# S5 scan with a rotation table of three planes, 512-column operations and states copied by ScalarE

## The chip, the cores and the metric

One core of a Trainium2 chip runs the whole program in one launch. The time is the device time of one execution in microseconds; for the kernel before, the median of three executions. A few per cent of a stretch's instructions may be missing in a trace, and starts and durations are those of one profiled execution.

## The reference

One inference step of a decoder trunk with four layers. The token mixers are S5 (layers 0 and 3), stick-breaking attention (layer 1) and a chunked gMLP (layer 2); behind each comes a SwiGLU FFN, and every sub-layer stands between two RMSNorms. A prompt of 512 positions and 8 sample tokens share all weights; the model has 1024 channels, and all values are fp32. The change concerns the S5 mixer alone:

```python
def s5_mixer(xn, w_in, lam_re, lam_im, log_dt, b_re, b_im, c_re, c_im, d_skip, w_glu, h0_re, h0_im):
    u = xn @ w_in                                  # 64 groups of 16 channels, 64 complex states each
    dt = exp(log_dt)
    ar, ai = exp(lam_re * dt) * cos(lam_im * dt), exp(lam_re * dt) * sin(lam_im * dt)
    br, bi = ...                                   # discretised b applied to u
    hr, hi = associative_scan(h[t] = a * h[t - 1] + b[t])          # complex, over the positions
    y = hr @ c_re - hi @ c_im + d_skip * u
    val, gate = split(gelu(y) @ w_glu)
    return val * sigmoid(gate), hr[-1], hi[-1]
```

## The kernel before

The class `Trunk` holds activations as 8 tiles of 128 channels x 520 columns (512 prompt positions, 8 sample tokens). A matmul with weights is made of three products in a reduced fp32 format (lines L235, L236, L238): the weights are loaded from DRAM (`raw`), ScalarE rounds them to `wh` (L206) and VectorE or GpSimd makes the rest `wl` (L208). These matmuls are most of the program. The instructions of every engine stand in a fixed order, which a scheduler writes with a timeline model of its own; in the source, tasks such as the S5 pipeline are generators that yield a number of microseconds of TensorE work (`S5Y`, `PREPY`, `STASH`) or a condition, and so are woven into the weight matmuls.

**S5.** `s5` (L994) projects the input; `u_evict` brings each tile of u out of PSUM (L1008, L1011) and copies its 8 sample columns to the end (L1012). `s5_pipe` (L786) then takes the 8 channel tiles through a pipeline. The 512 positions are cut into 64 chunks of 8. Stages of one tile:

- `powers_b` on GpSimd (L809 to L811; the first tile on VectorE), `powers_c` half on VectorE and half on GpSimd (L835 to L837): products of b and c with the powers of a inside a chunk (`ba`, `ca`). `kernels` (L839) makes the in-chunk kernel, writes it to one of two padded buffers `kpad`, stores it as `dk` (L854) and loads it back in shifted form as `wn` (L858).
- `inputs`: loads the tile's rotation table `rot` from DRAM (L862), spreads rho (L864), and makes the chunk weights `wi` from `ba` (matmuls L879, ScalarE L882).
- `chunks`: stores u (`du`, L887) and loads it in chunk form (`uq`, L890).
- `scan` (L894): 32 matmuls (L901) give the real and imaginary input of the 64 chunks for 4 blocks of 128 states in PSUM. VectorE multiplies them by the cosine (L909) and by the sine with real and imaginary part exchanged (L910), 512 columns each; combines them per part (L913, 256 columns each); runs a scan with real decay per part (L915); rotates back per part (L919, L920); and writes the states to `hm`, in four operations of 64 partitions x 256 columns (L925), while ScalarE copies the initial states there (L924). GpSimd takes the last states out (L926).
- `outputs` (L933, L934, ScalarE `ys` L938) and `finish` (L946, GELU into `zt` L950, then `xh` L393 and `xl` L394 for the GLU matmul).

In layer 0 all of this runs in the pipeline. For layer 3 (`kept`) `s5_stash` (L714) makes `wi`, `ca` and `wn` ahead, inside layer 2's FFN, and keeps them in DRAM; its pipeline loads them (L866 to L870). The `rot` tile in SBUF has one buffer in layer 0 and two in layer 3.

**Tables.** `s5_prep` (L603) makes the rotation table in 8 blocks of 4 state blocks, 64 columns each: an angle (VectorE L704 to L707), then ScalarE Abs (L708) and two Sin (L709, L710) for sine and cosine, in a tile `ro` with three buffers; each block is stored to DRAM (`rotd`, L711). Layer 0's tables are made at the start of the program, layer 3's inside the gMLP.

## Time and profile before

| | us |
|---|---|
| three executions | 2747.35, 2749.26, 2748.29 |
| median | 2748.29 |
| profiled execution | 2746.49 |
| its span, first to last instruction | 2744.8 |
| TensorE busy | 2576.6 (94%) |
| VectorE busy | 1545.9 (56%) |
| ScalarE busy | 1012.0 (37%) |
| GpSimd busy | 459.1 (17%) |
| mean granted TensorE clock | 0.968 of full speed |

The profiled execution is a single one, and its span is 1.7 us shorter than its own time. Busy shares are means over stages with different limits: what an engine's work is worth is read from the stretch in which it lies. The page cuts the span in 40 slices of 68.6 us (tenths of busy time, 9 is 90% or more); the first S5 layer's pipeline lies in the second and third slice, the second's in the 32nd and 33rd.

```profile
PE   7769999999998899999999989999999889999998
DVE  8883553434647854734345778565646755634344
ACT  5443333222344454432223564433324333432222
POOL 5661210000128820300000203000001111200000
```

PE is TensorE, DVE VectorE, ACT ScalarE and POOL GpSimd. SP in the orders below is SyncE, which issues the DMAs.

### The profile page before, as it was taken

Reading aid. Unit: us, or ns where it says so; the run is one execution under the profiler, and the core shown is the slowest. Engines: PE = TensorE matmul, PEld = TensorE weight load, DVE = VectorE, ACT = ScalarE, POOL = GpSimd, SP = SyncE. Lnnn points to the kernel's source line nnn. Section 1 sums busy time; section 2 is a strip of 40 time slices with the busy share of each in tenths; the row PEclk is TensorE's granted clock in tenths of the full one; section 3 lists DMA queues with packets and bytes.
Section 4 is the critical chain, followed back from the end, with each engine's and each line's share of the span. In section 5 each row is a group of like instructions: output and inputs, shape, how many; then the busy total and the mean of one; then the engine's idle time right before and its main releaser. Section 6 shows DMA issues by size and latency. Waiting matters only on the chain.

```text
span 2744.8 us, 49994 instructions
## 1 busy us (share of the span) xinstructions
PE 2576.6 (94%) x20922; PEld 2457.4 (90%) x20922; DVE 1545.9 (56%) x2703; ACT 1012.0 (37%) x1713; POOL 459.1 (17%) x487
## 2 busy tenths in 40 slices
PE   7769999999998899999999989999999889999998
PEld 6659999999986667999999889999999779999998
DVE  8883553434647854734345778565646755634344
ACT  5443333222344454432223564433324333432222
POOL 5661210000128820300000203000001111200000
PEclk8879999999999999999999999999999999999999
DMA  4533223333147643233333333344333544233331
GB/s 118 146 87 90 80 80 106 93 93 91 41 134 243 222 147 93 66 103 94 93 92 63 90 101 90 114 135 141 116 110 123 167 129 124 66 104 92 90 90 46
DMA packets 483073, 295.48 MB, mean 108 GB/s; under 512 B 52296, under 2 KB 458080, under 8 KB 482848
## 3 DMA queue, kind: packets, MB, share of 16 engines
q1 hardware_dynamic: 473632, 258.73, 33.1%
q0 software_dynamic: 9216, 33.56, 3.5%
q8 instruction: 165, 2.70, 0.4%
q14 instruction: 60, 0.49, 0.1%
HBM read 262.51 MB, written 29.72 MB: 106 GB/s over the span
## 4 chain that ended last, share of the span: by engine, by line
PE 73%; DVE 11%; DMA 5%; ACT 4%; POOL 3%; issue 2%; SPq 0%; ACTq 0%; DVEq 0%; POOLq 0%
PE pp L235 22%; PE pp L236 22%; PE pp L238 22%; POOL kp L1190 1%; DVE wl L208 1%; DMA raw<-in_w_ffn_in_dram 1%; DVE pn L423 1%; DVE x L425 1%; ACT wh L206 1%; PE pp L1338 1%; PE pp L1334 1%; DVE hm L925 1%; POOL x L425 1%; DMA rot<-rotd 1%; DMA wn<-wnd 1%
## 5 line engine op out<-in xcount | busy, mean ns | idle before, releaser
L235 PE MATMUL pp<-xh,wh 128*128 128x264 f32 (+1 forms) x4480 | 1209.0, 288 | 26.5 <-DVE u L1008 6.0
L236 PE MATMUL pp<-xl,wh 128*128 128x264 f32 (+1 forms) x4480 | 1210.6, 286 | 6.6 <-DVE xl L408 6.4
L238 PE MATMUL pp<-xh,wl 128*128 128x264 f32 (+1 forms) x4480 | 992.7, 286 | 6.2 <-POOL wl L208 5.6
L235 PEld LDWEIGHTS pp<-xh,wh 128*128 128x128 f32 x4480 | 853.5, 191 | 40.9 <-issue 14.1
L236 PEld LDWEIGHTS pp<-xl,wh 128*128 128x128 f32 x4480 | 854.5, 191 | 11.9 <-DVE xl L408 9.7
L206 ACT ACTIVATE wh<-raw 128x1024 fp32r<-128x1024 f32 (+2 forms) x384 | 391.3, 1023 | 1080.4 <-PE pp L236 724.7
L238 PEld LDWEIGHTS pp<-xh,wl 128*128 128x128 f32 x4480 | 738.7, 191 | 9.7 <-POOL wl L208 5.8
L208 DVE TENSOR_TENSOR wl<-raw,wh 128x1024 fp32r<-128x1024 f32 (+2 forms) x364 | 442.6, 1218 | 292.8 <-ACT wh L206 290.2
L236 PE MATMUL pp<-hl,wh 128*128 128x256 f32 (+1 forms) x1408 | 377.2, 283 | 0.0
L235 PE MATMUL pp<-hh,wh 128*128 128x256 f32 (+1 forms) x1408 | 376.7, 284 | 0.0
L238 PE MATMUL pp<-hh,wl 128*128 128x256 f32 (+1 forms) x1408 | 312.9, 283 | 0.0
L235 PEld LDWEIGHTS pp<-hh,wh 128*128 128x128 f32 x1408 | 265.1, 188 | 1.2 <-issue 1.2
L236 PEld LDWEIGHTS pp<-hl,wh 128*128 128x128 f32 x1408 | 265.3, 188 | 0.0
L238 PEld LDWEIGHTS pp<-hh,wl 128*128 128x128 f32 x1408 | 230.7, 188 | 0.0
L1622 DVE TENSOR_TENSOR tg<-pp,rs 128x520 f32<-128x520 f32 (+2 forms) x100 | 62.5, 632 | 215.4 <-PE pp L238 215.3
L1633 DVE TENSOR_TENSOR tg<-pp,tg 128x520 f32<-128x520 f32 (+2 forms) x96 | 62.4, 652 | 209.2 <-PE pp L238 208.6
L1645 DVE TENSOR_TENSOR op<-pp,op 128x520 f32<-128x520 f32 (+2 forms) x96 | 54.0, 563 | 168.1 <-PE pp L238 167.9
L340 POOL TENSOR_TENSOR acc<-acc,s 128x256 f32<-128x256 f32 (+1 forms) x96 | 83.7, 872 | 99.2 <-ACT s L336 95.3
L208 POOL TENSOR_TENSOR wl<-raw,wh 128x1024 fp32r<-128x1024 f32 x20 | 48.2, 2414 | 303.6 <-ACT wh L206 274.4
L407 ACT ACTIVATE xh<-x,gt 128x264 fp32r<-128x264 f32 (+1 forms) x128 | 63.0, 505 | 60.8 <-DVE x L425 42.5
L408 DVE SCALAR_TENSOR_TENSOR xl<-x,gt,xh 128x264 fp32r<-128x264 f32 (+1 forms) x128 | 76.7, 615 | 1.4 <-ACT xh L407 1.2
L336 ACT ACTIVATE sq<-op 128x256 f32<-128x256 f32 (+2 forms) x72 | 32.6, 453 | 101.4 <-DVE op L1645 68.4
...
## 6 DMA issues: line engine op xcount, KB each, us to landing
...
```

Source lines behind the costliest of these rows:

```text
L206: nc.scalar.activation(wh[:, :nk], raw[:, :nk], AF.Copy)
L208: on.tensor_tensor(wl[:, :nk], raw[:, :nk], wh[:, :nk], op=ALU.subtract)
L235: nc.tensor.matmul(ps(*h), lhsT=wh[:, k, :], rhs=xh[:, h[0]:h[1]], start=first, stop=False)
L236: nc.tensor.matmul(ps(*h), lhsT=wh[:, k, :], rhs=xl[:, h[0]:h[1]], start=False, stop=False)
L238: nc.tensor.matmul(ps(*h), lhsT=wl[:, k, :], rhs=xh[:, h[0]:h[1]], start=False, stop=last)
L340: i = (nc.gpsimd if pool else nc.vector).tensor_tensor(acc[0][:, c0:c1], acc[0][:, c0:c1], sq[:, :n], op=ALU.add)
L407: nc.scalar.activation(xs[k][0][:, c0:c1], self.x[k][:, c0:c1], AF.Copy, scale=g)
L408: return nc.vector.scalar_tensor_tensor(xs[k][1][:, c0:c1], self.x[k][:, c0:c1], g, xs[k][0][:, c0:c1], op0=ALU.mult, op1=ALU.subtract)
L425: add.tensor_tensor(self.x[k][:, c0:c1], self.x[k][:, c0:c1], t[:, :n], op=ALU.add)
L1622: v.tensor_tensor(g, ps(c0, c1), rs[:, c0:c1], op=ALU.mult)
L1633: v.tensor_tensor(t, ps(c0, c1), t, op=ALU.mult)
L1645: v.tensor_tensor(o, ps(c0, c1), o, op=ALU.add)
```

## The change

The rotation table gets a third plane, minus sine, so that both parts of a complex product can be formed by one operation over 512 columns.

- A table block is 128 x 768 instead of 128 x 512 (384 KB instead of 256), with one more ScalarE Sin per block; the tile `ro` has two buffers instead of three.
- `scan` multiplies by the cosine and by (sine, -sine), adds both parts in one operation, runs the two scans, multiplies by the cosine (512 columns), multiplies by (sine, -sine) in place in the table's tile (512) and adds that with the parts exchanged (512). Per tile, ten VectorE operations of 256 columns go and four of 512 come.
- A new stage `states`, at the head of the next round of the pipeline, copies the states to `hm` with four ScalarE copies of 64 x 256 per tile.
- One padded kernel buffer `kpad` instead of two; rho is spread over 63 columns of 64; u's 8-column copy goes from VectorE to ScalarE.

```diff
--- before.py
+++ after.py
@@ -127,9 +127,8 @@
 
         self.mod = c.tile([128, 16], F32, name="mod")
         nc.vector.tensor_reduce(self.mod, self.ident.rearrange("p (g q) -> p q g", q=16), axis=AX.X, op=ALU.add)
-        self.kpad = [c.tile([128, 256], F32, name=f"kpad{q}") for q in range(2)]
-        for q in range(2):
-            nc.gpsimd.memset(self.kpad[q][:, :128], 0.0)
+        self.kpad = [c.tile([128, 256], F32, name=f"kpad{q}") for q in range(1)]
+        nc.gpsimd.memset(self.kpad[0][:, :128], 0.0)
 
     def load_xt(self, tt):
         for t in tt:
@@ -579,7 +578,7 @@
         S["c"] = sp.tile([128, 2, 64, 16], F32, name="cn")
         S["h0"] = sp.tile([128, 2, 8, 32], F32, name="h0")
         S["rho"] = sp.tile([128, 32], F32, name="rho")
-        S["rot"] = self.dr.tile([128, 32, 2, 64], F32, tag="rot", name="rotd", bufs=1)
+        S["rot"] = self.dr.tile([128, 32, 3, 64], F32, tag="rot", name="rotd", bufs=1)
         p = S["tmp"] = self.tc.alloc_tile_pool(name="s5i", bufs=1, side="right")
         pin = p.tile([32, 3, 128], F32, name="pin")
         ldt = p.tile([32, 2], F32, name="ldt")
@@ -616,7 +615,7 @@
         dt = self.exp(p, prm[:, 2, :], 32, "dt")
 
         def rot_tile():
-            return p.tile([128, 512], F32, tag="ro", name="ro", bufs=3)
+            return p.tile([128, 768], F32, tag="ro", name="ro", bufs=2)
 
         def t32(name):
             return p.tile([128, 32], F32, name=name)
@@ -699,13 +698,15 @@
             yield PREPY[2]
             g = f8[:, 4 * b:4 * b + 4].unsqueeze(2).to_broadcast([128, 4, 64])
             it = self.iota[:, None, :].to_broadcast([128, 4, 64])
-            o = rot_tile().rearrange("p (a i c) -> p a i c", a=4, i=2)
-            n2, t = o[:, :, 0, :], o[:, :, 1, :]
+
+            o = rot_tile().rearrange("p (a i c) -> p a i c", a=4, i=3)
+            n2, t, m = o[:, :, 0, :], o[:, :, 1, :], o[:, :, 2, :]
             v.tensor_tensor(t, g, it, op=ALU.mult)
             v.tensor_scalar(n2, t, MAGIC, None, op0=ALU.add)
             v.tensor_scalar(n2, n2, MAGIC, None, op0=ALU.subtract)
             v.tensor_tensor(t, t, n2, op=ALU.subtract)
             nc.scalar.activation(n2, t, AF.Abs)
+            nc.scalar.activation(m, t, AF.Sin, scale=-TWO_PI_DOWN)
             nc.scalar.activation(t, t, AF.Sin, scale=TWO_PI_DOWN)
             nc.scalar.activation(n2, n2, AF.Sin, scale=-TWO_PI_DOWN, bias=self.hpi)
             nc.sync.dma_start(rot[:, 4 * b:4 * b + 4], o)
@@ -773,7 +774,7 @@
                 self.t += 0.3
                 if hf == 0:
                     yield STASH[1]
-            kp = self.kpad[t % 2]
+            kp = self.kpad[0]
             nc.scalar.activation(kp[:, 144:], ps[:, 16:128], AF.Copy)
             v.scalar_tensor_tensor(kp[:, 128:144], self.mod, self.gt[:, 128 + j * KT + t:129 + j * KT + t], ps[:, :16],
                                    op0=ALU.mult, op1=ALU.add)
@@ -846,7 +847,7 @@
                                      rhs=ca[:, 2 * a + g, 0:8].rearrange("p k c -> p (k c)"), start=g == 0, stop=g == 1,
                                      tile_position=(0, 32 * a))
             self.t += 0.6
-            kp = self.kpad[t % 2]
+            kp = self.kpad[0]
             nc.scalar.activation(kp[:, 144:], ps[:, 16:128], AF.Copy)
             v.scalar_tensor_tensor(kp[:, 128:144], self.mod, self.gt[:, 128 + j * KT + t:129 + j * KT + t], ps[:, :16],
                                    op0=ALU.mult, op1=ALU.add)
@@ -858,10 +859,10 @@
                 nc.sync.dma_start(wn[16 * r:16 * r + 16], dv[:, :, 128 - 16 * r:256 - 16 * r])
 
         def inputs(t):
-            rot_ = T[t]["rot"] = tp.tile([128, 4, 2, 64], F32, tag="rot", name="rot", bufs=1 + kept)
+            rot_ = T[t]["rot"] = tp.tile([128, 4, 3, 64], F32, tag="rot", name="rot", bufs=1 + kept)
             nc.sync.dma_start(rot_, rot[:, sl(t)])
             rho = T[t]["rho"] = tp.tile([128, 4, 64], F32, tag="rho", name="rho", bufs=1)
-            nc.scalar.activation(rho, S["rho"][:, sl(t)].unsqueeze(2).to_broadcast([128, 4, 64]), AF.Copy)
+            nc.scalar.activation(rho[:, :, 1:], S["rho"][:, sl(t)].unsqueeze(2).to_broadcast([128, 4, 63]), AF.Copy)
             gp.memset(rho[:, :, 0:1], 0.0)
             if kept:
                 wi = T[t]["wi"] = tp.tile([128, 2, 4, 128], F32, tag="wi", name="wi")
@@ -902,27 +903,33 @@
                                          rhs=uq[:, 2 * a + h // 64, 8:80], start=True, stop=True, tile_position=(0, h))
             self.t += 2.8
             sv = ps[:, :, :288].rearrange("p i (a c) -> p i a c", a=4)
-            cs, sn = rot_[:, :, 0, :], rot_[:, :, 1, :]
-            o1 = tp.tile([128, 2, 4, 64], F32, tag="o1", name="o1", bufs=1)
-            o2 = tp.tile([128, 2, 4, 64], F32, tag="o2", name="o2", bufs=1)
+            sh = [128, 2, 4, 64]
+            cs = rot_[:, :, 0, :].unsqueeze(1).to_broadcast(sh)
+            back = rot_[:, :, 1:3, :].rearrange("p a i c -> p i a c")
+            o1, o2 = (tp.tile(sh, F32, tag=f"o{q}", name=f"o{q}", bufs=1) for q in (1, 2))
+            v.tensor_tensor(o1, sv[:, :, :, 0:64], cs, op=ALU.mult)
+            v.tensor_tensor(o2, sv[:, ::-1, :, 0:64], back, op=ALU.mult)
+            nc.scalar.activation(S["ss"].rearrange("p i b a -> p i a b")[:, :, P, :], sv[:, :, :, 64:72], AF.Copy)
+            v.tensor_tensor(o1, o1, o2, op=ALU.add)
             rho = T[t]["rho"].rearrange("p a c -> p (a c)")
-            v.tensor_tensor(o1, sv[:, :, :, 0:64], cs.unsqueeze(1).to_broadcast([128, 2, 4, 64]), op=ALU.mult)
-            v.tensor_tensor(o2, sv[:, ::-1, :, 0:64], sn.unsqueeze(1).to_broadcast([128, 2, 4, 64]), op=ALU.mult)
-            nc.scalar.activation(S["ss"].rearrange("p i b a -> p i a b")[:, :, P, :], sv[:, :, :, 64:72], AF.Copy)
             for ri in range(2):
-                v.tensor_tensor(o1[:, ri], o1[:, ri], o2[:, ri], op=ALU.add if ri == 0 else ALU.subtract)
                 r = o1[:, ri].rearrange("p a c -> p (a c)")
                 v.tensor_tensor_scan(r, rho, r, 0.0, op0=ALU.mult, op1=ALU.add)
+            v.tensor_tensor(o2, o1, cs, op=ALU.mult)
+
+            v.tensor_tensor(back, o1, back, op=ALU.mult)
+            v.tensor_tensor(o2, o2, back[:, ::-1], op=ALU.add)
+            T[t]["h"] = o2
+
+        def states(t):
 
             hm = S["hm"][t % 2]
             for ri in range(2):
-                v.tensor_tensor(o2[:, 0], o1[:, ri], cs, op=ALU.mult)
-                v.tensor_tensor(o2[:, 1], o1[:, 1 - ri], sn, op=ALU.mult)
                 for g in range(2):
                     s = slice(64 * g, 64 * g + 64)
                     h = hm[64 * ri:64 * ri + 64, :, g]
-                    nc.scalar.activation(h[:, :, 0:8], S["h0"][s, ri].rearrange("p b a -> p a b")[:, P, :], AF.Copy)
-                    v.tensor_tensor(h[:, :, 9:73], o2[s, 0], o2[s, 1], op=ALU.subtract if ri == 0 else ALU.add)
+                    nc.scalar.activation(h[:, :, 0:8], S["h0"][s, ri].rearrange("p b a -> p a b")[:, sl(t), :], AF.Copy)
+                    nc.scalar.activation(h[:, :, 9:73], T[t]["h"][s, ri], AF.Copy)
             gp.tensor_copy(S["hf"][:, 8 * t:8 * t + 8], hm[:, :, :, 72].rearrange("p a g -> p (a g)"))
 
         def outputs(t):
@@ -970,6 +977,7 @@
         for q in [h[:, :, :, 8] for h in S["hm"]] + [S["bd"]]:
             gp.memset(q, 0.0)
         for t in range(-3, KT + 1):
+            stage(states, t)
             if t > -2 and not kept:
                 stage(powers_b, t + 2)
             if t > -1 and not kept:
@@ -1009,7 +1017,7 @@
                                 rs[:, c0:e].rearrange("p (c r) -> p c r", r=8), op=ALU.mult)
                 if c1 > NP:
                     v.tensor_tensor(u[:, 0:NS], ps(c0, c1)[:, NP - c0:], rs[:, NP:], op=ALU.mult)
-                    v.tensor_copy(u[:, NS + NP:], u[:, 0:NS])
+                    nc.scalar.activation(u[:, NS + NP:], u[:, 0:NS], AF.Copy)
                     ready.add(t)
             return f
         items = [(w_in, 0, t, u_evict(t)) for t in range(KT)]
```

Three places show how the order of instructions moves. In the changed kernel's rows line numbers are its own: L910 and L911 are the former L909 and L910, L917 the scans (L915), L918, L920 and L921 the rotation back, L836 to L838 the former L835 to L837, L393 the former L394.

VectorE in the first S5 layer, the scan of the sixth tile, before:

```order
L909 TENSOR_TENSOR o_1915<-pp,rot 128x512
L910 TENSOR_TENSOR o_1916<-pp,rot 128x512
L913 TENSOR_TENSOR o_1915<-o_1915,o_1916 128x256 x2
L915 SCALAR_TENSOR_TENSOR o_1915<-rho,o_1915 128x256 x2
L919 TENSOR_TENSOR o_1916<-o_1915,rot 128x256
L920 TENSOR_TENSOR o_1916<-o_1915,rot 128x256
L835 TENSOR_TENSOR ca<-cn,at 128x576
L925 TENSOR_TENSOR hm_737<-o_1916 64x4x64 x2
L837 TENSOR_TENSOR ca<-ca,tm 128x576
L919 TENSOR_TENSOR o_1916<-o_1915,rot 128x256
L920 TENSOR_TENSOR o_1916<-o_1915,rot 128x256
L925 TENSOR_TENSOR hm_737<-o_1916 64x4x64 x2
```

And in the changed kernel:

```order
L910 TENSOR_TENSOR o_1911<-pp,rot 128x512
L911 TENSOR_TENSOR o_1912<-pp,rot 128x512
L393 TENSOR_TENSOR xl_1338<-zt,xh_1337 128x520
L913 TENSOR_TENSOR o_1911<-o_1911,o_1912 128x512
L917 SCALAR_TENSOR_TENSOR o_1911<-rho,o_1911 128x256 x2
L852 SCALAR_TENSOR_TENSOR kpad_124<-mod,gt,psk 128x16
L918 TENSOR_TENSOR o_1912<-o_1911,rot 128x512
L920 TENSOR_TENSOR rot<-o_1911,rot 128x2x4x64
L921 TENSOR_TENSOR o_1912<-o_1912,rot 128x512
L836 TENSOR_TENSOR ca<-cn,at 128x576
L838 TENSOR_TENSOR ca<-ca,tm 128x576
```

The table (`rot`) was last read by the second L920, with two operations behind it in the tile; now its last reader is L921, the last operation of the tile, and L836 and L838 stand behind it.

ScalarE in the same layer, from the eighth tile's `rho` to the sample states (`ss`) of its scan, before:

```order
L864 ACTIVATE rho<-rho 128x256
L924 ACTIVATE hm_737<-h_160 64x4x8 x2
L938 ACTIVATE ys<-pp 72x8x8x16
L924 ACTIVATE hm_737<-h_160 64x4x8 x2
L882 ACTIVATE wi<-pp 128x1024
L950 ACTIVATE zt<-pp 128x8x64
L951 ACTIVATE zt<-pp 128x8
L393 ACTIVATE xh_1348<-zt 128x520
L911 ACTIVATE ss<-pp 128x2x4x8
```

In the changed kernel, from the copies of the sixth tile's states (L932) on:

```order
L932 ACTIVATE hm_743<-o_1912 64x4x64 x4
L931 ACTIVATE hm_742<-h_158 64x4x8 x2
L945 ACTIVATE ys<-pp 72x8x8x16
L931 ACTIVATE hm_742<-h_158 64x4x8 x2
L883 ACTIVATE wi<-pp 128x1024
L957 ACTIVATE zt<-pp 128x8x64
L958 ACTIVATE zt<-pp 128x8
L851 ACTIVATE kpad_124<-psk 128x112
L392 ACTIVATE xh_1339<-zt 128x520
L912 ACTIVATE ss<-pp 128x2x4x8
```

`wi` (L882, now L883), which the next scan's matmuls read, stood behind `ys` and the initial states; now the four copies of the states of the scan before stand ahead of it as well.

SyncE's queue where the first S5 layer begins; `raw` are weights, `rotd` the table in DRAM. Before:

```order
L196 DMA raw<-in_w_ssm_in_dram 128x8x128
L711 DMA rotd<-ro 128x512 x2
L196 DMA raw<-in_w_ssm_in_dram 128x8x128
L862 DMA rot<-rotd 128x512
L196 DMA raw<-in_w_ssm_glu_dram 128x8x128
L887 DMA du<-u 128x528
L196 DMA raw<-in_w_ssm_glu_dram 128x8x128
L890 DMA uq_732<-du 16x8x72
L890 DMA uq_732<-du 16x8x64 x6
L890 DMA uq_732<-du 16x8x72
```

In the changed kernel:

```order
L712 DMA rotd<-ro 128x768 x2
L195 DMA raw<-in_w_ssm_in_dram 128x8x128
L195 DMA raw<-in_w_ssm_glu_dram 128x8x128
L888 DMA du<-u 128x528 x4
L195 DMA raw<-in_w_ssm_glu_dram 128x8x128
L712 DMA rotd<-ro 128x768
L888 DMA du<-u 128x528
L195 DMA raw<-in_w_ssm_glu_dram 128x8x128
L712 DMA rotd<-ro 128x768
L888 DMA du<-u 128x528
L195 DMA raw<-in_w_ssm_glu_dram 128x8x128
L891 DMA uq_738<-du 16x8x64
```

All eight table blocks went out ahead of u's first store; now the last two go out behind four and five of these stores, and the first load of `rot` stands behind the first tile's `uq`. In the gMLP, VectorE's order now has the blocks of the second layer's table further apart: between the first and the last L704 stand 64 rows instead of 40.

## Rows read from the trace of the kernel before

**Rows 1.** Windows: stretch, length, busy us of each engine (instructions), PEclk, DMA share, GB/s

```profile
100.00:206.00 106.00, 71.75 (x702) 62.20 (x700) 94.57 (x133) 46.49 (x116) 71.38 (x62) 0.79 0.45 112
2160.00:2230.00 70.00, 53.26 (x590) 50.54 (x589) 55.22 (x117) 30.08 (x66) 2.09 (x14) 0.88 0.77 229
```

**Rows 2.** Groups of VectorE, first S5: busy us, mean ns | idle before, releasers

```profile
L925 DVE TENSOR_TENSOR hm<-o 64x256 f32<-64x256 f32 x32 | 20.9, 652 | 0.7
L915 DVE TENSOR_TENSOR_SCAN o<-rho,o 128x256 f32<-128x256 f32 x16 | 12.3, 801 | 0.0
L913 DVE TENSOR_TENSOR o<-o,o 128x256 f32<-128x256 f32 x16 | 11.6, 762 | 0.2
L920 DVE TENSOR_TENSOR o<-o,rot 128x256 f32<-128x256 f32 x16 | 10.1, 633 | 0.0
L919 DVE TENSOR_TENSOR o<-o,rot 128x256 f32<-128x256 f32 x16 | 9.5, 593 | 0.2
L837 DVE TENSOR_TENSOR ca<-ca,tm 128x576 f32<-128x576 f32 x6 | 9.3, 1556 | 0.1
...
L394 DVE TENSOR_TENSOR xl<-zt,xh 128x520 fp32r<-128x520 f32 x8 | 7.9, 988 | 6.4 <-ACT xh L393 6.3
L836 DVE TENSOR_TENSOR tm<-cn,at 128x576 f32<-128x576 f32 x6 | 5.7, 942 | 0.0
L909 DVE TENSOR_TENSOR o<-pp,rot 128x512 f32<-128x512 f32 x8 | 5.5, 690 | 12.8 <-DMA rot<-rotd 8.8 <-PE pp L901 3.9
L1012 DVE COPY u<-u 128x8 f32<-128x8 f32 x8 | 5.5, 703 | 0.0
```

**Rows 3.** Timeline of VectorE, first S5: start us, us, engine, line [idle before <-releaser]

```profile
130.28 0.68 DVE L909 TENSOR_TENSOR o<-pp,rot 128x512 f32<-128x512 f32 x1
...
149.03 0.69 DVE L909 TENSOR_TENSOR o<-pp,rot 128x512 f32<-128x512 f32 x1 [2.88 <-DMA rot<-rotd]
...
192.73 1.62 DVE L919 TENSOR_TENSOR o<-o,rot 128x256 f32<-128x256 f32 x1
194.27 1.48 DVE L920 TENSOR_TENSOR o<-o,rot 128x256 f32<-128x256 f32 x1
...
199.03 0.69 DVE L909 TENSOR_TENSOR o<-pp,rot 128x512 f32<-128x512 f32 x1 [2.37 <-DMA rot<-rotd]
...
208.75 0.69 DVE L909 TENSOR_TENSOR o<-pp,rot 128x512 f32<-128x512 f32 x1 [2.58 <-PE pp L901]
```

**Rows 4.** Timeline of GpSimd, the same stretch

```profile
147.13 1.05 POOL L810 TENSOR_TENSOR tn<-bbar,ap 128x512 f32<-128x512 f32 x1
...
192.15 1.91 POOL L837 TENSOR_TENSOR ca<-ca,tm 128x576 f32<-128x576 f32 x1
```

**Rows 5.** Chain of waits, first S5: start us, us, what

```profile
145.82 3.12 DMA rot<-rotd
```

**Rows 6.** Groups of VectorE, second S5

```profile
L925 DVE TENSOR_TENSOR hm<-o 64x256 f32<-64x256 f32 x32 | 14.0, 438 | 0.9
...
L394 DVE TENSOR_TENSOR xl<-zt,xh 128x520 fp32r<-128x520 f32 x6 | 4.2, 694 | 1.3 <-ACT xh L393 1.2
```

**Rows 7.** Groups of ScalarE, first S5

```profile
L882 ACT ACTIVATE wi<-pp 128x1024 f32<-128x1024 f32 x8 | 8.2, 1029 | 1.1 <-PE pp L879 1.0
L938 ACT ACTIVATE ys<-pp 72x1024 f32<-72x1024 f32 x8 | 8.2, 1021 | 4.9 <-PE pp L934 4.8
...
L864 ACT ACTIVATE rho<-rho 128x256 f32<-128x256 f32 x8 | 3.3, 414 | 13.3 <-DVE o L915 12.6 <-DMA rotd<-ro 0.6
```

**Rows 8.** Chain of waits, ahead of the first S5's pipeline

```profile
78.09 5.21 DMA rotd<-ro
```

**Rows 9.** Chain of waits, second S5

```profile
2216.22 1.93 PE pp L901 x32
```

**Rows 10.** Groups of VectorE, gMLP, the second layer's tables

```profile
L704 DVE TENSOR_TENSOR ro<-f,iota 128x256 f32<-128x256 f32 x8 | 3.2, 410 | 6.4 <-DMA rotd<-ro 6.4
```

**Rows 11.** Groups of ScalarE, the same stretch

```profile
L709 ACT ACT_TABLE_LOAD x5 | 6.4, 1283 | 0.1
```

## The prediction, made before the changed kernel ran

> **What bounds the kernel now.** I read the profile in this order. First the busy time of the engines over the whole span, which stands in the table of the profile: TensorE is busy for 94% of it, so VectorE work can be worth time only in a stretch in which TensorE idles. Then the windows of the two stretches that the change touches. In the first S5 layer [rows 1], from 100 to 206 us, TensorE is busy for 71.75 of 106 us and VectorE for 94.57; GpSimd, at 71.38, is busy too. The reader is to see that VectorE sets the pace there. In the second S5 layer TensorE is busy for 53.26 of 70 us, VectorE for only 55.22, GpSimd for almost nothing, and the DMA engines move 229 GB/s at a share of 0.77: that stretch runs on its loads.
>
> Then the groups of VectorE in the first S5 layer [rows 2]. They have one thing that matters: VectorE is hardly idle, except ahead of L909, the first operation of a tile's scan (12.8 us, 8.8 of it for the transfer of the rotation table). The table has a single buffer there, so its next tile is fetched when this tile's last multiply by it is done; one fetch takes 3.12 us [rows 5]. Last, the same operations with GpSimd idle, in the second layer [rows 6]: the 64x256 operation of L925 takes 438 ns instead of 652, and the 520-column L394 694 ns instead of 988. So a VectorE instruction is 0.2 to 0.3 us longer beside GpSimd, and this is about the same for 256 and for 520 columns: it goes by instructions. That is what speaks for fewer, longer ones.
>
> **The change, part by part.** The sum is made against the profiled execution, 2746.49 us, which lies 1.8 below the median of the runs, 2748.29.
>
> *Operations of the scan.* Per tile ten operations of 256 columns go: 2 x 0.762 (L913), 2 x 0.593 (L919), 2 x 0.633 (L920) and 4 x 0.652 (L925) = 6.58 us [rows 2]. Four of 512 columns in SBUF come. No row of this stretch has just that; the nearest is L394 with 520 columns, 0.988, which I take. The low end is the same operation beside an idle GpSimd, 0.694 [rows 6], the high end L837 with 576 columns, 1.556 [rows 2]. So 4 x 0.988 = 3.95 per tile; over eight tiles VectorE is busy for 21 us less (30 at the low end, 3 at the high one).
>
> *What of it lies on the path.* The starts of L909 run from 130.28 (third tile) to 199.03 (seventh) [rows 3]: four steps, 68.75 us. I walk through VectorE's order as it was before. From L909 to the last multiply by the table a tile needs 2 x 0.690 + 2 x 0.762 + 2 x 0.801 + 2 x 0.593 + 2 x 0.633 + 2 x 0.652 = 8.26, and more for what the order puts between (L836 and L835 at 0.942 each, L394, L837): 1.93, 4.43, 2.50 and 2.50 in the four steps. Behind it come the longer of the fetch (about 3.2 with its issue) and the work in its cover (3.80, 3.23, 3.23, 1.30). That makes 13.99 + 15.92 + 13.99 + 13.96 = 57.9. Measured were 68.75, of which 2.88 were a fetch held up ahead of 149.03 [rows 3, 5], which does not recur in the new queue order. The remaining 65.9 are 1.14 times the walk; the surplus is stalls beside GpSimd and short waits.
>
> The same walk in the new order: 2 x 0.690 + 4 x 0.988 + 2 x 0.801 = 6.93 to the table's last reader, with 2.50, 0.94, 4.43 and 0.99 between. The fetch is now longer, by 128 KB at 229 GB/s [rows 1] = 0.6, so 3.8; and since the last operation of the tile is now the table's last reader, little is left to cover it. That is 13.23 + 11.67 + 15.16 + 11.72 = 51.8, times 1.14 = 59.0. Against 68.75 this is **-9.8**.
>
> *The copies on ScalarE.* Four of 64x256, at the 0.414 of L864 [rows 7], are 1.66 us per tile; ScalarE is busy for 46.49 of 106 us [rows 1], so its busy time hides them. But its queue is in order: for the seventh and eighth tile the new order puts these copies and `ys` ahead of `wi`, which the next scan's matmuls need. The path from the end of one scan to the next is then 1.66 + 1.02 + 1.03 [rows 7] + 1.93 of matmuls (L901, [rows 9]) = 5.6, where the fetch alone would be 3.8. In the step to the seventh tile that is 1.8 x 1.14 = **+2.1**. In the last step, where GpSimd has run dry, VectorE needs 2 x 0.690 + 5 x 0.694 + 2 x 0.801 = 6.5, and 5.6 behind it: 12.1 against the 9.72 from 199.03 to 208.75 [rows 3], **+2.4**.
>
> *First two steps.* They lose 2 x 2.63 of operations and two copies of L1012 at 0.703 (moved to ScalarE): -6.7. The fetch is longer by 0.6 each, and one of them loses the 1.3 of L925 and some of u's evictions as cover: +2.7. Together **-4.0**.
>
> *Start of the pipeline.* The last two table blocks go out behind u's first stores. Before, the last block's write took 5.21 and landed at 83.30 [rows 8], some 18 us ahead of the first scan; now it is half as long again and later, while u's evictions come earlier. I take **+1.5** between -3 and +10.
>
> *Second S5 layer.* Its VectorE work shrinks by 10 x 0.438 - 4 x 0.694 = 1.6 per tile [rows 6], of which a loop that runs on loads gives little back; at most five tiles' worth, -8. Its table loads grow by 0.6 per tile, +4.6 if all eight lie on the path. I take **+1.5**. The last tile's states now come from four ScalarE copies of 1.66 instead of two pairs of L925, and the shorter chain ahead pays for it.
>
> *The second layer's tables, in the gMLP.* Eight more Sin operations (0.414 each by the nearest row, [rows 7]) are +3.3; in ScalarE's new order two table loads of 1.283 [rows 11] fewer, -2.6. VectorE's waits for a free table buffer, 6.4 us now [rows 10], could grow with two buffers instead of three, but the order also spreads the blocks out. Taken **+0.5**, between -4 and +13 (below).
>
> *At nothing:* one padded kernel buffer instead of two (a tile needs it once in some 15 us, its store is covered by that), 63 instead of 64 columns of rho, u's wrap copy on ScalarE. If that cover went, the next tile's kernel would wait for that store to land.
>
> Sum: -9.8 + 2.1 + 2.4 - 4.0 + 1.5 + 1.5 + 0.5 = -5.8, so 2740.7 for a profiled execution and, with 1.8, **2742** for the median. About 0.2%, 5.5 us, is what a measurement can tell from no change: the forecast lies at that border.
>
> **The rivals.**
>
> *Stalls go wholly by instructions.* Then a 512-column operation costs 0.694 and nothing is to be scaled: the four steps take 51.8 - 16 x 0.294 = 47.1 against 65.9, -18.8. With +2.1, -4.0, +2.4 and +3.5 of the rest that is -14.8, or 2733. For it speaks that the surplus of L394 (0.29) is hardly more than that of L925 (0.21). Against it: GpSimd's own work, 71.38 us in that stretch [rows 1], does not shrink, and the powers it makes are needed tile by tile.
>
> *The two engines take turns.* Beside GpSimd's L837, which starts at 192.15 and takes 1.91 [rows 4], VectorE's L919 and L920 take 1.62 and 1.48 [rows 3] instead of some 0.4: each runs in the gap that the other leaves. If what counts is then the sum of both engines' SBUF work, a tile has 9 x 1.05 of GpSimd [rows 4] and on VectorE 10 x 0.438 + 2 x 0.801 + 3 x 0.942 + 0.694 = 9.5; that becomes 7.9. From 18.95 to 17.35, so the four steps take 0.916 x 65.9 = 60.3, -5.6 instead of -9.8, and the first two -2.3 in proportion. Sum: -5.6 + 2.1 - 2.3 + 2.4 + 3.5 = +0.1, or 2748. The Trainium skill, page "SBUF — State Buffer", section "Who interferes with whom", states a rule of this kind: VectorE and GpSimd share a pair of ports under an exclusive lock, and an operation with two SBUF inputs blocks a GpSimd one that reads SBUF. The alternation in the rows agrees for single instructions. Against the rival: 18.95 is more than the 16.5 that a tile takes, so not everything excludes everything.
>
> *Slower, by the two table buffers.* In the gMLP, VectorE issues the blocks in its own queue, in order; with two buffers six of the eight first operations (L704) must wait for the write two blocks back, and the evictions that TensorE needs stand behind them. Three such waits are 6.4 us now, 2.13 each [rows 10]; by bytes 1.5 times as long, 3.2. Six make 19.2, +12.8 against now. Instead of +0.5 the sum is +6.5, or 2755. It decides from waits of 3.0 on average (6 x 3.0 - 6.4 = +11.6, the whole then at +5.3). For it: the single queue, and 5.21 for a write of 256 KB [rows 8]. Against it: the blocks stand further apart in the new order.
>
> That the change doesn't do what it says would mean that the operations with a reversed or repeated plane run at a lower rate; L909, which repeats a plane, takes 0.690 for 512 columns [rows 2], like any other, so I give it nothing of its own.
>
> **How the numbers follow.** Forecast 0.54, of which 0.27 lie beyond 0.2% faster, 0.23 within it and 0.04 slower, since its own range is 2735 to 2750. Wholly by instructions 0.19, all faster. Taking turns 0.12: 0.01 faster, 0.08 within, 0.03 slower. Two buffers 0.15, all slower. Faster 0.47, same 0.31, slower 0.22. The range has to take in the first rival with part of the loads' gain of the second layer (2728) and the last one with an unlucky start (2758): 2728 to 2758.
>
> **What would show it.** Right: the four 512-column operations at about 1.0 us in the first S5 layer and 0.7 in the second; L909's successors 14 to 15 us apart between the third and the seventh tile; VectorE idle for about 3.8 us ahead of each, and for TensorE ahead of the last two; the second S5 layer as long as before or a little longer. The first rival is right if the operations stay at 0.7 in the first layer too. The second, if they take 1.3 or more and GpSimd's powers release the scans. The last, if L704 idles for over 15 us for the table's writes. The prediction is wrong if the steps of the first S5 layer do not shrink, or if the layer's start moves by more than 5 us.

## The result and the profile after

The changed kernel took 2762.19 us in the median of five executions (2757.03 to 2771.42), the kernel before, in five runs of its own, 2749.26 (2747.35 to 2753.62): a ratio of 1.0051, with a 95% interval of 1.003 to 1.0071. It is slower by 0.5%, some 14 us (8 to 20), where 6 us faster had been forecast (2742 against 2748.29). The profiled execution took 2760.18 us against 2746.49, so its 13.7 us can be followed.

What the change set out to do happened. In the two windows of the S5 layers VectorE is busy for 81.08 us instead of 94.57, and for 46.30 instead of 55.22 [rows 1]; TensorE did less in the first, 66.61 instead of 71.75. The windows are the same in time for both kernels, while the changed kernel's scans lie 7 to 8 us later in them, so a small part of these differences is that shift. The windows of the changed kernel (columns as in rows 1):

```profile
100.00:206.00 106.00, 66.61 (x688) 57.24 (x688) 81.08 (x89) 61.12 (x159) 71.73 (x72) 0.79 0.47 111
2160.00:2230.00 70.00, 54.52 (x587) 51.26 (x586) 46.30 (x70) 38.69 (x87) 1.89 (x13) 0.90 0.79 241
```

The groups of VectorE in the first S5 layer (columns as in rows 2):

```profile
L917 DVE TENSOR_TENSOR_SCAN o<-rho,o 128x256 f32<-128x256 f32 x16 | 14.5, 945 | 0.4
L920 DVE TENSOR_TENSOR rot<-o,rot 128x512 f32<-128x512 f32 x8 | 11.5, 1442 | 0.0
...
L921 DVE TENSOR_TENSOR o<-o,rot 128x512 f32<-128x512 f32 x8 | 9.1, 1137 | 0.1
L918 DVE TENSOR_TENSOR o<-o,rot 128x512 f32<-128x512 f32 x8 | 9.0, 1120 | 0.1
...
L393 DVE TENSOR_TENSOR xl<-zt,xh 128x520 fp32r<-128x520 f32 x8 | 8.1, 1014 | 10.1 <-ACT xh L392 10.1
...
L913 DVE TENSOR_TENSOR o<-o,o 128x512 f32<-128x512 f32 x8 | 6.5, 807 | 0.2
...
L910 DVE TENSOR_TENSOR o<-pp,rot 128x512 f32<-128x512 f32 x8 | 5.5, 690 | 22.2 <-PE pp L902 14.5 <-DMA rot<-rotd 7.7
```

Four 512-column operations stand in the place of ten of 256 columns. They take 807, 1120, 1442 and 1137 ns (L913, L918, L920, L921), together 36.1 us instead of 52.1 for what they replace. But VectorE is now idle for 22.2 us ahead of a scan (L910) instead of 12.8 [rows 2], 14.5 of it for TensorE's matmuls (L902).

The first scan of the kernel before, and some of the scans of the changed kernel, in the first layer:

```profile
101.62 0.69 DVE L909 TENSOR_TENSOR o<-pp,rot 128x512 f32<-128x512 f32 x1 [1.33 <-PE pp L901]
```

```profile
108.77 0.69 DVE L910 TENSOR_TENSOR o<-pp,rot 128x512 f32<-128x512 f32 x1 [2.00 <-PE pp L902]
...
138.75 0.69 DVE L910 TENSOR_TENSOR o<-pp,rot 128x512 f32<-128x512 f32 x1 [2.91 <-DMA rot<-rotd]
...
197.78 0.69 DVE L910 TENSOR_TENSOR o<-pp,rot 128x512 f32<-128x512 f32 x1 [5.73 <-PE pp L902]
...
211.64 0.69 DVE L910 TENSOR_TENSOR o<-pp,rot 128x512 f32<-128x512 f32 x1 [6.77 <-PE pp L902]
```

The reader is to see three stretches. The first scan starts at 108.77 instead of 101.62: 7.1 us late. From the third to the seventh tile it takes 59.03 us instead of 68.75 [rows 3]: 9.7 gained. The last step takes 13.86 instead of 9.72, and the engine waits 6.77 ahead of it. From the first scan to the last this is 102.87 us instead of 107.13, a gain of 4.3 in all; the last scan starts 2.9 us late.

By the same marks in both traces, the rest: to the last `ys` of the layer 1.6 us more are lost, to the GLU's first gate 3.0, to the end of the mixer 2.3, which makes 9.8. Up to the gMLP 1.7 are lost, in the gMLP 3.1 and in its FFN 2.0 are won, and the second S5 layer loses 7.1: the changed kernel is 6.3 behind at its head, 13.4 at its end.

These are single executions. The experiments t10 and t12 below are one kernel, and their traces agree within 1.3 us in each stretch of the first S5 layer, but are 5.5 us apart between that layer and the gMLP (1182.4 and 1176.9) and 1.4 in the gMLP and in its FFN. So the 1.7 up to the gMLP and the 2.0 of the FFN are no more than such spread. The gMLP's gain is more: it takes 175.2 to 177.0 us in the five kernels with the changed kernel's table blocks (the changed one, t1, t2, t6, t7) and 178.3 to 181.8 in the nine others.

### The profile page after: what moved, and what is told of

It reads as the page before. It is cut to its first block, busy times and chain, and to the rows that moved or that the text cites. A ratio compares the mean times of both kernels' runs of the same rounds, so it can differ in the third digit from the quotient of the medians.

```text
span 2758.5 us, 50010 instructions
## 1 busy us (share of the span) xinstructions
PE 2573.5 (93%) x20922; PEld 2453.4 (89%) x20922; DVE 1518.1 (55%) x2591; ACT 1042.7 (38%) x1807; POOL 459.7 (17%) x486
## 4 chain that ended last, share of the span: by engine, by line
PE 72%; DVE 13%; DMA 5%; ACT 5%; issue 2%; POOL 2%; SPq 0%; ACTq 0%; DVEq 0%; POOLq 0%
PE pp L234 22%; PE pp L235 21%; PE pp L237 21%; DVE wl L207 2%; DMA raw<-in_w_ffn_in_dram 1%; ACT wh L205 1%; POOL kp L1198 1%; DVE pn L422 1%; DVE x L424 1%; PE pp L1346 1%; PE pp L1342 1%; DMA raw<-in_w_ssm_glu_dram 1%; DVE o L917 1%; DVE xl L407 1%; POOL x L424 1%
```

## The experiments

In diffs, `-` and `+` are against the kernel that the text names. All ratios are to runs of the kernel before on the same chip. "First scan" is the first L909 (or its successor), "scans" the time from the first to the eighth, "gate" the time from the last `ys` to the first `sg` of the GLU, in the first and second S5 layer. t5, t6 and t7 have one execution each: it shows where time lies, not what the edit is worth on the whole.

| run | ratio to before (interval) | first scan | scans 1 | gate 1 | gate 2 |
|---|---|---|---|---|---|
| before | 1 | 101.62 | 107.13 | 19.8 | 19.8 |
| changed | 1.0051 (1.003 to 1.0071) | 108.77 | 102.87 | 22.8 | 22.3 |
| t1 | 1.0012 (0.9995 to 1.0028) | 109.25 | 106.35 | 19.8 | 19.8 |
| t2 | 1.0012 (1.0001 to 1.0022) | 108.57 | 102.74 | 19.8 | 19.9 |
| t3 | 1.0026 (1.0014 to 1.0038) | 99.72 | 103.19 | 23.5 | 22.1 |
| t4 | 1.0016 (1.0003 to 1.0029) | 101.79 | 104.31 | 19.8 | 19.9 |
| t5 | one execution | 108.79 | 104.49 | 19.8 | 19.8 |
| t6 | one execution | 107.52 | 99.96 | 19.8 | 22.5 |
| t7 | one execution | 108.41 | 103.00 | 23.3 | 21.4 |
| t8 | 0.9999 (0.9986 to 1.0012) | 101.19 | 103.21 | 22.4 | 19.8 |
| t9 | 1.0011 (1.0002 to 1.002) | 102.19 | 100.72 | 19.8 | 19.8 |
| t10 | 0.997 (0.9961 to 0.998) | 101.26 | 102.51 | 19.8 | 19.9 |
| t11 | 1.0012 (1.0001 to 1.0023) | 102.23 | 105.93 | 19.8 | 19.9 |
| t12 | 0.9972 (0.9962 to 0.9983) | 101.91 | 101.81 | 19.8 | 19.9 |

### What delays the first scan: t1 and t5

t1 is the kernel before with the new table (and the single padded kernel buffer) alone; the main lines of its edit:

```diff
-            return p.tile([128, 512], F32, tag="ro", name="ro", bufs=3)
+            return p.tile([128, 768], F32, tag="ro", name="ro", bufs=2)
...
+            nc.scalar.activation(m, t, AF.Sin, scale=-TWO_PI_DOWN)
...
-            rot_ = T[t]["rot"] = tp.tile([128, 4, 2, 64], F32, tag="rot", name="rot", bufs=1 + kept)
+            rot_ = T[t]["rot"] = tp.tile([128, 4, 3, 64], F32, tag="rot", name="rot", bufs=1 + kept)
```

> The kernel before with the changed kernel's table alone: three planes, 128x768 blocks in two buffers, 384 KB fetched per tile, one padded kernel buffer; the scan and the states stay as before. If the table is what delays the first S5 layer's start (A), the first tile's scan starts some 5 to 8 us later than before's 101.62, its operations and steps are those of before (about 60 us from the second to the sixth step's end, a little longer by the fetch), and the whole is 5 to 10 us slower than before. If the start came late for another reason (the evictions of u or the ScalarE copies), the first scan starts within 2 us of before's and the whole is within 3 us.

The first scan came at 109.25, as A said. The whole was some 3 us slower and not 5 to 10, with an interval that takes in no change: the gMLP, in which VectorE waits for no table buffer (0.0 us instead of 6.4), gave back 2.4 us (176.6 instead of 179.0).

t5 is the kernel before with one buffer less, and nothing else:

```diff
-            return p.tile([128, 512], F32, tag="ro", name="ro", bufs=3)
+            return p.tile([128, 512], F32, tag="ro", name="ro", bufs=2)
```

> The kernel before with one edit: the table's tile has two buffers instead of three, blocks and planes as before. If the second buffer's loss alone delays the table's last store (A1), the first scan starts 4 to 8 us later than 101.62, since the last two blocks go out behind u's first stores here too. If it is the third plane (longer stores, one more Sin), the first scan starts within 2 us of 101.62.

108.79: it is the buffer, not the third plane. The order of SyncE had the last two blocks behind u's first stores, and the trace shows who waits for them. ScalarE's first instruction of the pipeline (`rho`) in the kernel before, and the last table stores of SyncE and the same instruction in the changed kernel:

```profile
83.47 0.42 ACT L864 ACTIVATE rho<-rho 128x256 f32<-128x256 f32 x1 [0.63 <-DMA rotd<-ro]
```

```profile
90.63 0.32 SPq L712 DMA_DIRECT2D rotd<-ro  x1
...
92.38 1.89 SPq L712 DMA_DIRECT2D rotd<-ro  x1
```

```profile
99.87 0.41 ACT L865 ACTIVATE rho<-rho 128x252 f32<-128x252 f32 x1 [3.02 <-DMA rotd<-ro]
```

`rho` does not read the table, yet it waits for the last block's store: the pipeline's tiles lie in the memory that the table's blocks leave. So the pipeline's first instruction on ScalarE starts at 83.47 before and at 99.87 now, and GpSimd's first (it clears `uq`) 0.1 and 0.3 us behind it; the load of `uq` for the first scan follows.

### The states on ScalarE: t2, t3, t4

t2 is the changed kernel with the copies on VectorE:

```diff
-                    nc.scalar.activation(h[:, :, 9:73], T[t]["h"][s, ri], AF.Copy)
+                    v.tensor_copy(h[:, :, 9:73], T[t]["h"][s, ri])
```

> The changed kernel with the four 64x256 copies of the states on VectorE instead of ScalarE. If the copies on ScalarE cost what the last steps and the GLU lost (B): the last two steps of the scans shrink from 15.4 and 13.9 to about 13 and 11 us, the pause of 4.4 us ahead of the first GLU gate is gone in both S5 layers (there the rounding of four weights stands ahead of it on ScalarE), and the whole is 8 to 14 us below the changed kernel; the late start of the first scan (108.8) stays. If VectorE's time is what counts there, the four copies lengthen each step by 1 to 2.5 us instead and the whole is no faster than the changed kernel.

B holds on the whole: against the changed kernel's 1.0051 it is 1.0012, some 11 us, and the two intervals do not touch. Of the last two steps only the last one shrank, to 11.92; the step to the seventh tile is 15.86. The gate is back at 19.8 in both layers.

t3 is the changed kernel, but it makes the minus plane when a tile's table is loaded, so that the table keeps two planes and three buffers:

```diff
-            return p.tile([128, 768], F32, tag="ro", name="ro", bufs=2)
+            return p.tile([128, 512], F32, tag="ro", name="ro", bufs=3)
...
-            nc.scalar.activation(m, t, AF.Sin, scale=-TWO_PI_DOWN)
...
-            nc.sync.dma_start(rot_, rot[:, sl(t)])
+            nc.sync.dma_start(rot_[:, :, 0:2, :], rot[:, sl(t)])
+            nc.scalar.activation(rot_[:, :, 2, :], rot_[:, :, 1, :], AF.Copy, scale=-1.0)
```

> The changed kernel with a table of two planes as before (256 KB per tile, blocks of 128x512 in three buffers); the minus-sine plane is made when a tile's table is loaded, by one ScalarE copy with scale -1 (some 0.4 us). If the table delays the start (A): the first scan starts at about 102 us instead of 108.8 and the whole is 5 to 8 us below the changed kernel. If the start has another cause, it stays at 107 or later, and the whole is within 3 us of the changed kernel or above it by the added copies.

A holds for the start: 99.72. On the whole it is some 7 us below the changed kernel, with two intervals that overlap at their ends.

t4 takes the edits of t2 and t3 together.

> Both: the minus plane made at load and the states copied by VectorE. If A and B are two separate costs, they add: 13 to 22 us below the changed kernel, that is from 2740 to 2750, level with before or up to 8 us faster by the gain of the four steps in the middle. If they share a cause, it is no better than the better of the two alone.

The two do not add: 1.0016 is no better than t2. The start is good in t4 (101.79), and the first S5 layer ends level with before's, 4.1 us ahead of t2's; but with the table of before the gMLP takes 181.7 us instead of t2's 175.4. So the new table is two things that nearly cancel: a late start, and a shorter gMLP. What keeps both t2 and t4 above the kernel before is in part the second S5 layer, where VectorE's copies put 4.7 us more between the last scan and its `ys` (15.6 and 15.5 instead of 10.8).

### The GLU's first gate: t6 and t9

In the changed kernel ScalarE has four weight roundings (`wh`) between the last `ys` and the first gate (`sg`), and waits 6.00 and 5.29 us for the loads of weights ahead of the second and the third; before it had one. ScalarE in the kernel before and in the changed one, from these roundings to the gate:

```profile
237.71 1.06 ACT L206 ACTIVATE wh<-raw 128x1024 fp32r<-128x1024 f32 x1 [13.76 <-PE pp L236]
...
240.08 0.60 ACT L1077 ACTIVATE sg<-pp 128x520 f32<-128x520 f32 x1
```

```profile
230.83 1.06 ACT L205 ACTIVATE wh<-raw 128x1024 fp32r<-128x1024 f32 x1 [2.13 <-DMA out_im_s_dram<-so]
237.90 1.06 ACT L205 ACTIVATE wh<-raw 128x1024 fp32r<-128x1024 f32 x1 [6.00 <-DMA raw<-in_w_ssm_glu_dram]
244.24 2.00 ACT L205 ACTIVATE wh<-raw 128x1024 fp32r<-128x1024 f32 x2 [5.29 <-DMA raw<-in_w_ssm_glu_dram]
...
247.56 1.10 ACT L1085 ACTIVATE sg<-pp 128x520 f32<-128x520 f32 x2
```

TensorE, the matmul that waited for that gate, before and in the changed kernel, and windows of the changed kernel around it (columns as in rows 1):

```profile
240.74 0.39 PE L235 MATMUL pp<-xh,wh 128*128 128x256 f32 x1 [1.16 <-ACT sg L1077]
```

```profile
248.21 0.58 PE L234 MATMUL pp<-xh,wh 128*128 128x256 f32 x1 [4.36 <-ACT sg L1085]
```

```profile
240.00:245.00 5.00, 3.85 (x33) 3.64 (x31) 0.21 (x1) 0.76 (x1) 0.00 (x0) 1.00 0.35 105
...
246.00:248.00 2.00, 0.00 (x0) 0.00 (x0) 1.69 (x2) 1.97 (x3) 0.00 (x0) 0.59 0.08 22
248.00:253.00 5.00, 4.79 (x22) 4.79 (x23) 1.90 (x2) 2.45 (x5) 0.00 (x0) 0.50 0.72 201
253.00:255.00 2.00, 2.00 (x18) 2.00 (x18) 1.03 (x2) 0.96 (x1) 0.00 (x0) 0.95 0.29 62
255.00:260.00 5.00, 5.00 (x44) 5.00 (x43) 2.78 (x4) 1.59 (x2) 0.00 (x0) 1.00 0.66 188
```

TensorE stands for 4.36 us. In that time the granted clock falls, and the first 5 us of matmuls run at 0.50, the lower of its two levels: 22 matmuls from 248 to 253, where 44 run in 5 us at 1.00. In the second S5 layer the pause is 3.83 us and the clock 0.71 in the mean of the 5 us behind it.

The 14 traces have 28 such places. In the 20 with one rounding ahead of the gate, the gate comes after 19.8 us and TensorE waits 1.2; in the 8 with four, it comes after 21.4 to 23.5 and TensorE waits 3.0 to 4.9. t8 below, in which ScalarE copies no states at all, is among the 8 with its first layer: it is the order that goes with the loss, whichever edit brings it about.

t6 is the changed kernel with the states of the last three tiles copied by VectorE. With it the order ahead of the gate differs between the two layers of one kernel.

```diff
-                    nc.scalar.activation(h[:, :, 9:73], T[t]["h"][s, ri], AF.Copy)
+                    if t >= 5:
+                        v.tensor_copy(h[:, :, 9:73], T[t]["h"][s, ri])
+                    else:
+                        nc.scalar.activation(h[:, :, 9:73], T[t]["h"][s, ri], AF.Copy)
```

> The changed kernel with the states of the tiles 6 to 8 copied by VectorE and of 1 to 5 by ScalarE. By this the order of ScalarE ahead of the GLU's first gate is the one of before in the first S5 layer (one weight rounding ahead of it) and that of the changed kernel in the second (four). If that order is what the GLU's loss hangs on (C), the time from the last ys to the first gate is about 19.8 us in the first layer and about 22.3 in the second, and TensorE's pause of over 4 us appears in the second alone. If the loss comes from the copies themselves, both layers have 22 or both 20.

C holds: 19.8 in the first layer, 22.5 and a pause of 3.53 in the second. t9 is the kernel of t3 with VectorE's copies for the last tile alone:

```diff
-                    nc.scalar.activation(h[:, :, 9:73], T[t]["h"][s, ri], AF.Copy)
+                    if t >= 7:
+                        v.tensor_copy(h[:, :, 9:73], T[t]["h"][s, ri])
+                    else:
+                        nc.scalar.activation(h[:, :, 9:73], T[t]["h"][s, ri], AF.Copy)
```

> The kernel of t3 (minus plane made at load, states on ScalarE) with one edit: the last tile's four copies of the states are made by VectorE. The order of ScalarE ahead of the GLU's first gate is then that of before in both S5 layers (one weight rounding, where t3 has four). If this order is what the GLU loses by (C), the time from the last ys to the first gate falls from 23.5 and 22.1 to about 19.8 in both layers, the GLU behind it loses its stretch at half the clock, and the whole is 7 to 12 us below t3: 2745 to 2750. If the order is only a companion of another loss, those times stay above 22 or the whole changes by less than 4 us.

The gates are 19.8 in both layers, as C said, and from the last `ys` to the end of the layer t9 takes 6.2 and 5.1 us less than t3. The whole is only some 4 us below t3 rather than 7 to 12, with intervals that overlap; in the first layer t9 gives 2.4 us of it back between the last scan and the last `ys` (14.7 instead of 12.4). So the loss at the gate is shown where it arises, and its worth in the whole only roughly.

### Is VectorE's wait for the copies on the path: t7

In the second S5 layer of the changed kernel VectorE waits for the copies, since the next tile's multiply by sine writes the tile that they read:

```profile
L911 DVE TENSOR_TENSOR o<-pp,rot 128x512 f32<-128x512 f32 x8 | 5.5, 687 | 6.9 <-ACT hm L932 6.9
```

t7 is the changed kernel with a second buffer for that tile (`o2`) in that layer:

```diff
-            o1, o2 = (tp.tile(sh, F32, tag=f"o{q}", name=f"o{q}", bufs=1) for q in (1, 2))
+            o1, o2 = (tp.tile(sh, F32, tag=f"o{q}", name=f"o{q}", bufs=q if kept else 1) for q in (1, 2))
...
-                so = pools["t"].tile([128, 2, 4, 64], F32, tag="o2", name="so", bufs=1)
+                so = pools["t"].tile([128, 2, 4, 64], F32, tag="o2", name="so", bufs=2 if "wi" in S else 1)
```

> The changed kernel with a second buffer for the scan's result (o2) in the second S5 layer, so that the next tile's multiply by sine need not wait for ScalarE's copies of the states. If that wait (6.9 us of idle VectorE ahead of L911, put down to the copies) is on the path (D), the eight scans of the second layer take 60 us or less from first to last instead of 64.6. If the layer runs on its loads anyway, the wait moves to the table's or the inputs' transfer and the span stays within 1.5 us of 64.6.

D falls: the scans take 65.9 us, and the wait has moved to the matmuls ahead of L910:

```profile
L910 DVE TENSOR_TENSOR o<-pp,rot 128x512 f32<-128x512 f32 x8 | 5.5, 689 | 15.6 <-PE pp L902 11.8 <-DMA rot<-rotd 3.8
...
L911 DVE TENSOR_TENSOR o<-pp,rot 128x512 f32<-128x512 f32 x8 | 5.4, 679 | 0.0
```

### Whose turn it is: t8, t10, t11, t12

t8 leaves the table and the states as they were before and edits the rotation back alone. The product with sine goes to PSUM, in the scan's own tile (`sv` is its view):

```diff
-            for ri in range(2):
-                v.tensor_tensor(o2[:, 0], o1[:, ri], cs, op=ALU.mult)
-                v.tensor_tensor(o2[:, 1], o1[:, 1 - ri], sn, op=ALU.mult)
+            o3 = sv[:, :, :, 0:64]
+            v.tensor_tensor(o3, o1[:, ::-1], sn.unsqueeze(1).to_broadcast(sh), op=ALU.mult)
+            v.tensor_tensor(o2, o1, cs.unsqueeze(1).to_broadcast(sh), op=ALU.mult)
...
-                    v.tensor_tensor(h[:, :, 9:73], o2[s, 0], o2[s, 1], op=ALU.subtract if ri == 0 else ALU.add)
+                    v.tensor_tensor(h[:, :, 9:73], o2[s, ri], o3[s, ri], op=ALU.subtract if ri == 0 else ALU.add)
```

> The kernel before (table of two planes in three buffers, states written by VectorE) with one edit in the scan: the rotation back is made by two operations of 512 columns instead of four of 256, the product with sine goes into the scan's own PSUM tile, and the four operations that write the states take one operand from there. If fewer instructions with two SBUF operands are what helps beside a busy GpSimd, the scans of the first layer take 97 to 103 us from first to last instead of 107, with the start of before, and the whole is 3 to 8 us faster than before, less some 5 us if ScalarE's order ahead of the GLU turns out as in the changed kernel (in the first layer it does). If instructions on both engines simply take turns, the scans stay within 2 us of 107.

The scans took 103.2 us, and the whole was level with before: the GLU's order was the bad one in the first layer (gate 22.4). The groups of VectorE in its first S5 layer show more than the time:

```profile
L913 DVE TENSOR_TENSOR o<-o,o 128x256 f32<-128x256 f32 x16 | 15.6, 1017 | 0.2
L915 DVE TENSOR_TENSOR_SCAN o<-rho,o 128x256 f32<-128x256 f32 x16 | 14.6, 941 | 0.0
L927 DVE TENSOR_TENSOR hm<-o,pp 64x256 f32<-64x256 f32 x32 | 13.4, 419 | 0.5
```

L927, which writes the states with one operand in PSUM, takes 419 ns, as it does in the second layer beside an idle GpSimd; before, with both operands in SBUF, it took 652 and 438. But L913 and L915, which are not edited, rose from 762 and 801 to 1017 and 941 [rows 2]. For L913 this is a stall that has moved: it takes 727 to 857 in the four kernels with the scan of before (before, t1, t5, t11) and 1017 to 1043 in t8, t10 and t12. For L915 it is not clear, since it takes 801 to 1015 in those four. Summed over L913, the scans and the operations behind them, the first layer's busy time less the second's, where GpSimd idles, is 60.2 - 41.1 = 19.1 us in t8 (18.1 and 18.2 in t10 and t12), 64.4 - 43.7 = 20.7 in the kernel before (25.3 in t1 and t5, 23.7 in t11), and 50.6 - 32.2 = 18.4 in the changed one. So a good part of the stall stays, and some of it goes.

t10 is t8 with u's 8-column copies on ScalarE, which the changed kernel has too. t11 is the kernel before with these copies alone, and t12 is t10 again, beside t11.

```diff
-                    v.tensor_copy(u[:, NS + NP:], u[:, 0:NS])
+                    nc.scalar.activation(u[:, NS + NP:], u[:, 0:NS], AF.Copy)
```

> The kernel of t8 (rotation back by two operations, product with sine in PSUM, table as before) with u's 8-column copies on ScalarE. The order ahead of the GLU's gate is that of before in both layers. If t8 lost by that order in the first S5 layer what its scans had gained (107 to 103), the whole is now 4 to 9 us below before. If GpSimd's turns limit the layer, VectorE's lighter load gives nothing: within 3 us of before.

> The kernel before with u's 8-column copies on ScalarE alone (table, scan and states as before). If what made t10 faster is this edit, the whole is again 6 to 10 us below before. If it is the rotation back with one operand in PSUM together with an undisturbed GLU order, this one is within 3 us of before, since the copies take VectorE 5.5 us in the first S5 layer, of which most lies ahead of the pipeline.

> The kernel of t10 once more, beside t11 on the same chip: 5 to 11 us below before if t10's result holds, level with t11 if the u copies are the cause.

t10 is faster than before by 0.30% (0.20 to 0.39), and again by 0.28% (0.17 to 0.38); the u copies alone are not (1.0012). The gate comes after 19.8 in both layers of all three. So t10 is faster than the kernel before by some 8 us and than the changed one by some 22, by the ratios. Its first S5 layer ends 6.8 us ahead of before's, 6.1 in t12.

## Why the prediction was wrong

In the prediction's own terms three steps failed. The hand-over to the GLU was not in the sum, without a reason, and cost some 9 us in the two layers. The start was taken at +1.5 and measured 7.1. And the gain of the scan, -9.3 over its seven steps (-4.0, -9.8, +2.1 and +2.4), measured -4.3.

**The scan: about half of what was forecast, and its largest term came out by luck.** The four steps in the middle were forecast at -9.8, with +2.1 for ScalarE: -7.7. They measured -9.7. But t1 and t5, which keep the scan of before and start as late as the changed kernel, take 63.62 and 62.26 us for these four steps, 5.1 and 6.5 less than 68.75. Against them the changed kernel's 59.03 is a gain of 4.6 and 3.2, and of 3.5 and 1.6 over all seven steps (102.87 against 106.35 and 104.49). The third and the seventh scan in t5:

```profile
139.25 0.68 DVE L909 TENSOR_TENSOR o<-pp,rot 128x512 f32<-128x512 f32 x1
...
201.51 0.69 DVE L909 TENSOR_TENSOR o<-pp,rot 128x512 f32<-128x512 f32 x1 [2.95 <-PE pp L901]
```

So most of the -9.7 goes with the later start, and not with fewer and longer operations. The walk itself hid this: with the measured prices of the operations and scans (1.127 and 0.945) its four tiles come to 55.2 instead of 51.8, and the factor of 1.14, which was to cover stalls, covered them a second time. The last step was forecast at +2.4 and came at +4.1 (13.86 instead of 9.72). t2, which has no ScalarE copies, takes 11.92 for it, so the path through the copies, `ys` and `wi` to the matmuls is worth 1.9; t1, t5 and t11, with the states written as before, take 11.8 to 12.1, so the 9.72 was short. In the step to the seventh tile the copies cost nothing: 15.44, and 15.86 without them.

**First two steps: -4.0 forecast, +1.3 measured** (29.98 instead of 28.66). Here the start is what failed the forecast, and not the price of the lighter scan. With the start of before, in t3, t4 and t9, the changed scan takes 26.50, 25.51 and 25.07, that is 2.2 to 3.6 less (their fetches are the shorter ones of before). With the late start the scan of before takes 30.46 (t5) and 30.60 (t1). GpSimd is busy for 24.32 us of these two steps in the changed kernel and 23.29 in t5, but for 17.85 in the kernel before and 17.79 in t3: with the late start, these tiles meet more of its work. The prediction let the start move and priced the steps as if it had not. The windows of these two steps (columns as in rows 1) in the kernel before, the changed one, t5 and t3:

```profile
101.62:130.28 28.66, 21.32 (x230) 19.55 (x230) 25.95 (x41) 12.56 (x29) 17.85 (x17) 0.89 0.65 170
```

```profile
108.77:138.75 29.98, 21.78 (x234) 18.82 (x235) 24.86 (x26) 17.80 (x42) 24.32 (x20) 0.87 0.52 122
```

```profile
108.79:139.25 30.46, 21.06 (x212) 18.71 (x213) 30.05 (x37) 12.95 (x26) 23.29 (x21) 0.84 0.38 101
```

```profile
99.72:126.22 26.50, 20.00 (x230) 18.39 (x231) 22.31 (x26) 12.99 (x31) 17.79 (x17) 0.92 0.77 197
```

**Start of the pipeline: +1.5 forecast, +7.1 measured, within its bounds of -3 to +10.** The last two blocks' place in SyncE's queue was read from the order, but not who waits for them: the first instructions of the pipeline, for the memory. t5 shows that the lost buffer alone does it.

**The GLU was not in the sum at all.** Some 9 us, 5.3 in the first layer and 3.8 in the second, come with four roundings ahead of the first gate on ScalarE, the pause of TensorE and the lower clock behind it. The prediction looked at three places of the order, and not at the place where the layer hands over to the next stage. t6 and t9 show it, by moving a few tiles' copies.

**Second S5 layer: +1.5 forecast, +7.1 measured, outside the bounds of -8 to +4.6.** The scans themselves went from 65.13 to 64.55, as near to nothing as was said. The rest lies around them: the first scan comes 1.9 us later behind the layer's head (35.7 instead of 33.7, where t8 to t12 have 33.8 to 35.2), the last tile's states 2.0 later (forecast: paid for), and the GLU takes the remainder.

**gMLP: +0.5 forecast, -3.1 measured.** The rival with two table buffers fell with its sign: VectorE does not wait for them at all there.

```profile
L704 DVE TENSOR_TENSOR ro<-f,iota 128x256 f32<-128x256 f32 x8 | 3.2, 416 | 0.0
```

The same group had 6.4 us of waits before [rows 10]. With two buffers and blocks of the old size, in t5, it has 7.3 us, far from the 19.2 that the rival asked for.

**The price of an operation, and the first two rivals.** 0.988 was taken for 512 columns; the mean was 1.127. Beside an idle GpSimd, in the second layer, they take 0.683 to 0.691. The first layer's surplus is 17.6 to 18.4 us for these operations and the scans, six a tile, in three kernels that leave the states to ScalarE (changed, t3, t7), against 20.7 to 25.3 for the twelve of before (before, t1, t5, t11): half the instructions bear some three quarters of the stall. "Stalls go wholly by instructions" falls. "The two engines take turns" asked for 1.3 a piece, and only L920 reached it; its reason, that stall goes with the other engine's work, is borne out in part by t8, where the stall taken from L927 came back on L913. Of the two instructions from which this rival was read, L920 (from 194.27) begins when GpSimd's L837 has ended (194.06), and stands beside the next one. Both rivals' gains were also reckoned from 65.9, and the forecast's from 68.75; from the same base they would have been -21.6 and -8.4 instead of -18.8 and -5.6. The Trainium skill, page "SBUF — State Buffer", section "Who interferes with whom", says that a VectorE instruction with at most one input from SBUF, outside the modes that use two ports, does not contend with GpSimd. L927 agrees: 419 ns with GpSimd busy and with GpSimd idle.

**What would have been right.** The sum, without the GLU and with the measured start, is -5.8 + 5.6 = -0.2: no change. The 13.7 us of the profiled execution add up from 7.1 at the start, some 9 around both GLUs and 5.5 in both layers' last tiles (1.6 and 2.0 to `ys`, and 1.9 at the second one's head), less the scans' 4.9 and the 5.1 of gMLP and FFN; the remainder of 2 us lies in stretches that the change does not touch, within the spread of single executions there. What makes the scheduler put four roundings ahead of the gate stays open.
